# Down projection of a SwiGLU block: eight of eleven row pairs as seven block products instead of eight

## The chip, the cores and the metric

The kernel runs on one core of a Trainium2 chip. The metric is the device time of one execution in microseconds (us); the time before is 926.69 us, the median of three runs that lie between 925.08 and 927.98 us. The core has a matrix engine (TensorE, PE in the profile, with its weight loads as PEld), VectorE (DVE), ScalarE (ACT), GpSimd (POOL) and SyncE (SP), which issues most DMA transfers. TensorE multiplies a stationary 128x128 operand by a moving one of up to 512 columns and adds the product up in PSUM banks of 128x512 fp32; the other engines work from SBUF and PSUM.

## The reference

One encoder layer on 512 tokens of width 1024, in fp32, then a final RMS norm:

```
h  = rms_norm(x, g_mix);  z = h @ w_in            # gates, latent q/kv, mLSTM streams, memory queries
merged = g0 * (o_mla @ w_branch[0]) + g1 * (o_ml @ w_branch[1]) + g2 * (o_mem @ w_branch[2])
x  = x + merged @ w_out
h2 = rms_norm(x, g_ffn)
x  = x + (silu(h2 @ w_ffn_gate) * (h2 @ w_ffn_up)) @ w_ffn_down      # 1024 -> 2816 -> 1024
out = rms_norm(x, g_final)
```

`o_mla` is latent attention (8 heads), `o_ml` a bidirectional mLSTM, `o_mem` attention to 256 memory tokens. The change concerns the last product, `act @ w_ffn_down`: 512 tokens by 2816 by 1024. Its 2816 rows are 22 tiles of 128, taken as 11 pairs ("chunks").

## The kernel before

**Precision.** Every product of two fp32 matrices is made of three fp32r matmuls: each operand is split into a high part (ScalarE copies it into fp32r, L85 or L88) and a low part (VectorE subtracts, L86 or L89), and `mm3` (L101 to L106) adds high x high, low x high and high x low in one bank. `wload` (L91) loads a weight tile of 128x1024 through a raw tile and splits it; raw tiles have two buffers, split ones three.

**Stages.** First the memory keys, then memory attention and mLSTM, then the latent projections (`latent_units`, L703) and latent attention (`mla_units`, L774). Beside these the generator `fill` supplies gate and branch products (`merge_branch`, L225). There the tiles of `merged` are summed: branch product times gate on VectorE (L242), and the sum into `merged` on GpSimd (L243). Then follow the output projection, the second norm, and the feed-forward stage (L947 to L1022), which writes its 22 activation tiles: the first six (`EARLY`) stay in SBUF split, the other sixteen go to a DRAM tile `act_dr`. The first three feed-forward tiles are plain products; the other nineteen (`ffn_first` to `ffn_third`) already use seven block products where eight would be plain, with sums of weight blocks made on VectorE.

**Down projection.** `projection` (L893) takes the two column halves of 512 in turn. In each half every chunk gives, for each of four token tiles, two row tiles of three matmuls: 24 matmuls with 512 columns. The activation is the stationary operand, the weight the moving one. In half 0 `act_load` (L1036) fetches the two activation tiles of a chunk and splits them. In half 1 the last three chunks' weights are kept (`wd_t`) so that each token tile can be finished, normalised and stored in turn (`store`, L1055); there the last token tile is done in two pieces of 256 columns.

**Order of the work.** The program is written as loops; a planner replays it on a timeline of its own and fixes from that each engine's order, preferring what is written first among what is ready. Engines then take their instructions strictly in that order and wait on semaphores. SBUF tiles live in pools that are laid over one another in time: a tile in a new pool must wait for the last use of the old tiles at its place. The pools touched here are `fs`, `ht` and `fg` (feed-forward work tiles, `th` and `u` in `fs`), released at L1023, and `fin` (L1027), which takes their place.

Of the kernel before, what the change touches and what calls it, by code (L numbers as in the profile page):

```python
# [11 lines left out]
F32 = mybir.dt.float32  # L12
F32R = mybir.dt.float32r
I32 = mybir.dt.int32
AF = mybir.ActivationFunctionType
# [22 lines left out]
EARLY = 6  # L38
NEG = -1.0e30
# [21 lines left out]
def block_kernel(ctx, tc, x, mem, pos, inv, g_mix, mem_g, g_ffn, g_final, g_q, g_kv, gate_bias,  # L61
# [17 lines left out]

    def bcast_rows(t, src):  # L80
        nc.gpsimd.dma_start(out=t, in_=src.partition_broadcast(P))
# [26 lines left out]
    def bank(pool):  # L108
        return pool.tile([P, 512], F32, name=pool.name, tag=pool.name)

    def rsqrt_mean(pool, ss, n, count, tag):
# [3 lines left out]
        nc.gpsimd.tensor_tensor(out=r, in0=v, in1=mhalf[:, :n], op=ALU.pow)  # L115
        return r
# [61 lines left out]
    with ExitStack() as mix:  # L178
# [46 lines left out]
        def merge_branch(order, b, o_hi, o_lo, ths, spare=None):  # L225
# [6 lines left out]
            for m in range(KD):  # L232
# [236 lines left out]
        act_mark = []  # L469
# [85 lines left out]
        def head(pr, u, hn):  # L555
# [5 lines left out]
            def make(j):  # L561
                e = lp.tile([P, 640], F32, name="e", tag="e", bufs=3)
                nc.sync.dma_start(out=e, in_=a_dr[h, j].partition_broadcast(P))
# [270 lines left out]

        run(latent_units(), fill, 0.0)
# [3 lines left out]
        run(mla_units(oa_hi, oa_lo), fill, 0.9)  # L839
# [188 lines left out]
    act_hi = fin.tile([P, NF - EARLY, S], F32R, name="act_hi")  # L1028
    act_lo = fin.tile([P, NF - EARLY, S], F32R, name="act_lo")

    def act_side(c):
        if 2 * c < EARLY:
            return early[0], early[1], 2 * c
        return act_hi, act_lo, 2 * c - EARLY

    def act_load(c):  # L1036
        for f in (2 * c, 2 * c + 1):
            if f >= EARLY:
                a = acte.tile([P, S], F32, name="act", tag="act", bufs=2)
                nc.sync.dma_start(out=a, in_=act_dr[f - EARLY])  # L1040
                split(act_hi[:, f - EARLY], act_lo[:, f - EARLY], a, scale=-0.5)

    last = tc.alloc_tile_pool(name="last", bufs=1, side="right")
    wd_t = [[last.tile([P, 1024], F32R, name=f"wd{c}{i}") for i in range(2)] for c in range(3)]
# [4 lines left out]
    def hold_down(lead):  # L1049
        return [wload(w_fd[1, c], into=wd_t[c - lead]) for c in range(lead, NF // 2)]  # L1050

    def gain_low(t):
        nc.gpsimd.tensor_tensor(out=xg[t][:, :H], in0=x2[t][:, :H], in1=gfin_b[:, :H], op=ALU.mult)

    def store(t, r):  # L1055
        rows = slice(t * P, (t + 1) * P)
        A.activation(xg[t][:, :H], xg[t][:, :H], AF.Copy, scale=r)
        nc.scalar.dma_start(out=out[rows, :H], in_=xg[t][:, :H])
        n = H // 2 if t == NT - 1 else H
        for c0 in range(H, D, n):  # L1060
            cols = slice(c0, c0 + n)
# [86 lines left out]
```

## Time and profile before

| | us |
|---|---|
| median of three runs | 926.69 |
| profiled execution, its own time | 925.3 |
| its span | 923.4 |
| TensorE busy | 905.1 |
| VectorE busy | 636.1 |
| ScalarE busy | 509.2 |
| GpSimd busy | 85.2 |

The profile is of one execution. Busy time of TensorE counts overlapping matmuls once, and the granted clock is 0.999 of full speed over the span. A group row gives what an engine did at one line: how often, how long in total and on average, and what ended the idle time ahead of it. A timeline row gives start, length and engine of an instruction (or of several like it, with their count), and in brackets how long the engine idled before and what released it. The profiled execution is 1.39 us below the median.

### The profile page before, as it was taken

Reading aid. Unit: us, or ns where it says so; the run is one execution under the profiler, and the core shown is the slowest. Engines: PE = TensorE matmul, PEld = TensorE weight load, DVE = VectorE, ACT = ScalarE, POOL = GpSimd, SP = SyncE. Lnnn points to the kernel's source line nnn. Section 1 sums busy time; section 2 is a strip of 40 time slices with the busy share of each in tenths; the row PEclk is TensorE's granted clock in tenths of the full one; section 3 lists DMA queues with packets and bytes.
Section 4 is the critical chain, followed back from the end, with each engine's and each line's share of the span. In section 5 each row is a group of like instructions: output and inputs, shape, how many; then the busy total and the mean of one; then the engine's idle time right before and its main releaser. Section 6 shows DMA issues by size and latency. Waiting matters only on the chain.

```text
span 923.4 us, 13931 instructions
## 1 busy us (share of the span) xinstructions
PE 905.1 (98%) x5282; PEld 787.7 (85%) x5282; DVE 636.1 (69%) x1088; ACT 509.2 (55%) x896; POOL 85.2 (9%) x139
## 2 busy tenths in 40 slices
PE   7998999999999999999999999999999999999997
PEld 5987787878888788888888879999999999988886
DVE  5768968888684856677553855989898988354323
ACT  8565676686653456677574445545454545244222
POOL 2001002121111101001000500000000000000200
PEclk9999999999999999999999999999999999999999
DMA  7421244434432122121224250423434431365322
GB/s 274 161 75 47 77 133 125 157 121 140 140 111 92 50 86 83 40 87 60 78 69 160 90 191 17 160 93 125 149 115 127 159 115 69 105 225 162 106 76 91
DMA packets 36675, 104.82 MB, mean 114 GB/s; under 512 B 5169, under 2 KB 7537, under 8 KB 36609
## 3 DMA queue, kind: packets, MB, share of 16 engines
q1 hardware_dynamic: 34560, 99.65, 32.4%
q0 software_dynamic: 1184, 3.24, 1.0%
q10 hardware_dynamic: 864, 1.06, 0.3%
q8 instruction: 41, 0.67, 0.3%
q14 instruction: 26, 0.21, 0.1%
HBM read 97.55 MB, written 6.37 MB: 113 GB/s over the span
## 4 chain that ended last, share of the span: by engine, by line
PE 90%; DVE 4%; DMA 2%; ACT 1%; issue 1%; POOL 0%; POOLq 0%; DVEq 0%; SPq 0%; ACTq 0%
PE pg L104 17%; PE pg L106 17%; PE pg L105 17%; PE po L104 7%; PE po L106 7%; PE po L105 7%; PE psc L104 2%; PE psc L105 2%; PE psc L106 2%; PE ptp L818 2%; DVE w_lo L86 1%; PE ppv L588 1%; PE ppv L587 1%; DMA raw<-w_out_d 1%; PE ppv L586 1%
## 5 line engine op out<-in xcount | busy, mean ns | idle before, releaser
L86 DVE TENSOR_TENSOR w_lo<-raw,w_hi 128x1024 fp32r<-128x1024 f32 (+3 forms) x112 | 126.0, 1127 | 92.4 <-ACT w_hi L85 90.7
L104 PE MATMUL pg<-h_hi,w_hi 128*128 128x512 f32 (+1 forms) x476 | 175.2, 369 | 0.8 <-DVE q_lo L89 0.6
L105 PE MATMUL pg<-h_lo,w_hi 128*128 128x512 f32 (+1 forms) x476 | 175.6, 369 | 0.0
L106 PE MATMUL pg<-h_hi,w_lo 128*128 128x512 f32 (+1 forms) x476 | 175.1, 368 | 0.3 <-DVE w_lo L86 0.3
L85 ACT ACTIVATE w_hi<-raw 128x1024 fp32r<-128x1024 f32 (+3 forms) x112 | 107.0, 958 | 104.4 <-PE pg L105 57.2
L104 PEld LDWEIGHTS pg<-h_hi,w_hi 128*128 128x128 f32 x476 | 89.6, 188 | 15.4 <-DVE q_lo L89 0.8
L106 PEld LDWEIGHTS pg<-h_hi,w_lo 128*128 128x128 f32 x476 | 89.5, 188 | 14.8 <-DVE w_lo L86 0.7
L105 PEld LDWEIGHTS pg<-h_lo,w_hi 128*128 128x128 f32 x476 | 89.5, 188 | 13.7
L571 ACT ACTIVATE e<-e,ccol 128x512 f32<-128x512 f32 (+3 forms) x64 | 32.3, 554 | 28.2 <-DMA e<-a_dr 27.6
L1073 DVE TENSOR_REDUCE nm<-psc 128x1 f32<-128x512 f32 (+1 forms) x48 | 27.7, 596 | 19.9 <-PE psc L106 19.5
L576 DVE TENSOR_TENSOR e<-e,psc 128x512 f32<-128x512 f32 (+3 forms) x64 | 29.1, 482 | 17.5 <-POOL e L574 14.6
L1076 ACT ACTIVATE pn<-psc,nm 128x512 f32<-128x512 f32 (+1 forms) x48 | 29.4, 614 | 17.6 <-DVE nm L1073 17.6
L85 ACT ACTIVATE w_hi<-rawab 128x1024 fp32r<-128x1024 f32 x19 | 20.1, 1059 | 29.0 <-PE pg L105 17.4
L574 POOL TENSOR_SCALAR_AFFINE_SELECT e<-e 128x128 f32<-128x128 f32 x64 | 24.0, 384 | 121.5 <-ACT e L571 110.2
L104 PE MATMUL po<-h_hi,w_hi 128*128 128x256 f32 (+1 forms) x116 | 33.8, 291 | 1.4 <-ACT w_hi L85 1.4
L86 DVE TENSOR_TENSOR w_lo<-rawab,w_hi 128x1024 fp32r<-128x1024 f32 x19 | 23.2, 1222 | 16.1 <-ACT w_hi L85 16.0
L1079 ACT ACTIVATE pn<-pn,rs 128x512 f32<-128x512 f32 (+1 forms) x48 | 29.8, 651 | 7.7 <-DVE rs L1078 7.5
L105 PE MATMUL po<-h_lo,w_hi 128*128 128x256 f32 (+1 forms) x116 | 33.7, 290 | 0.0
L106 PE MATMUL po<-h_hi,w_lo 128*128 128x256 f32 (+1 forms) x116 | 33.6, 290 | 0.0
L86 DVE TENSOR_TENSOR s_lo<-e,s_hi 128x640 fp32r<-128x640 f32 x32 | 26.1, 825 | 4.3 <-ACT s_hi L85 2.6
L105 PE MATMUL po<-w_lo,act_hi 128*128 128x512 f32 (+1 forms) x74 | 27.4, 375 | 0.0
L85 ACT ACTIVATE w_hi<-s 128x1024 fp32r<-128x1024 f32 x19 | 20.1, 1059 | 12.9 <-PE pg L105 9.9
(511 smaller groups left out, 2565.3 us busy)
## 6 DMA issues: line engine op xcount, KB each, us to landing
raw<-w_zt_d SPq DMA_DIRECT2D x46, 512.0 KB, 3.4
raw<-w_fd_d SPq DMA_DIRECT2D x22, 512.0 KB, 3.4
e<-a_dr SPq DMA_DIRECT2D x32, 320.0 KB, 3.4
rawab<-w_fg_d SPq DMA_DIRECT2D x19, 512.0 KB, 3.8
rawab<-w_fu_d SPq DMA_DIRECT2D x19, 512.0 KB, 4.7
raw<-w_br_d SPq DMA_DIRECT2D x12, 512.0 KB, 3.5
raw<-w_out_d SPq DMA_DIRECT2D x8, 512.0 KB, 3.6
act_dr<-u SPq DMA_DIRECT2D x16, 256.0 KB, 3.9
```

What stands on the lines that cost most here:

```text
L85: A.activation(hi, src, AF.Copy)
L86: V.tensor_tensor(out=lo, in0=src, in1=hi, op=ALU.subtract)
L104: mm(ps, wh, ah, start=start and i == 0, stop=False, skip_group_check=more)
L105: mm(ps, wh, al, start=False, stop=False, skip_group_check=more)
L106: mm(ps, wl, ah, start=False, stop=stop and i == n - 1, skip_group_check=more)
L571: A.activation(e[:, c0:c0 + n], e[:, c0:c0 + n], AF.Exp, bias=ccol[:, j, d, row:row + 1])
L574: nc.gpsimd.affine_select(out=dg, in_=dg, pattern=[[sgn, P]], compare_op=ALU.is_ge, fill=0.0, base=0, channel_multiplier=-sgn)
L576: V.tensor_tensor(out=e[:, c0:c0 + n], in0=e[:, c0:c0 + n], in1=sc[:, t0:t0 + n], op=ALU.mult)
L818: nc.tensor.transpose(tp[:, c * 256 + q * P:c * 256 + (q + 1) * P], pn[q][:, (kt + c) * P:(kt + c + 1) * P], ident)
L1073: nc.vector.tensor_reduce(out=nm, in_=sc, axis=AX.X, op=ALU.max, negate=True)
L1076: nc.scalar.activation(pn, sc, AF.Exp, bias=nm, accum_out=sm)
L1079: nc.scalar.activation(pn, pn, AF.Copy, scale=rs)
```

## The change

Eight of the eleven chunks (chunks 3 to 10) are computed as 2x2 block products: the tokens are cut into two halves of 256, a chunk's 256 rows into its two row tiles, the 1024 columns into two halves. The usual eight block products become seven, on sums of blocks. Three loops over the eight chunks do two, three and two of them, with banks `px`, `py`, `pz`, `pw`; the three early chunks (`C0`) stay plain and stand between the loops. `onto` adds a finished or half-finished bank to the residual `x2`.

The four sums of weight blocks per chunk are made by DMA in DRAM: four plain copies on SP's queue (placed after the last load of the mLSTM's `e` tiles), then on GpSimd's queue two accumulating transfers of 2 MB, two copies and two accumulating transfers of 1 MB, two copies and two more accumulating transfers. The sums of activation blocks (`d`) are four 128x256 VectorE operations a chunk. The activations are no longer kept split; they are loaded once (one block a second time) and split per loop. Raw weight tiles lie alternately in `stage` and in `fin`; three chunks' weights are loaded a second time at the end. The sum into `merged` moves from GpSimd to VectorE.

```diff
@@ merge_branch
-                    nc.gpsimd.tensor_tensor(out=merged[:, m], in0=merged[:, m], in1=th, op=ALU.add)
+                    V.tensor_tensor(out=merged[:, m], in0=merged[:, m], in1=th, op=ALU.add)
@@ beside mla_units
+        def down_sums():
+            groups = range(2)
+            low, high = ([w_fd[u, C0 + 4 * g:C0 + 4 * g + 4] for g in groups] for u in range(2))
+            with tc.issue_after(load_mark[0]):
+                for g in groups:
+                    nc.sync.dma_start(out=t13[g][:, :, 0], in_=low[g][:, :, 0:512])
+                    nc.sync.dma_start(out=t13[g][:, :, 1], in_=high[g][:, :, 512:1024])
+            yield
+            def add(t, src):
+                with tc.issue_after(pool_mark[0]):
+                    nc.gpsimd.dma_start(out=t, in_=src, accum_op=ALU.add)
+            for g in groups:
+                add(t13[g], high[g][:, :, 0:512].unsqueeze(2).to_broadcast([4, P, 2, 512]))
+                yield
...
-        run(mla_units(oa_hi, oa_lo), fill, 0.9)
+        run(beside(mla_units(oa_hi, oa_lo), down_sums()), fill, 0.9)
@@ down projection
+    def acts(c):
+        ab = (acte if c == 0 else fin).tile([P, 2, S], F32, name="ab", tag="ab", bufs=1 if c == 0 else 3)
+        for i in range(2):
+            nc.sync.dma_start(out=ab[:, i], in_=act_dr[2 * c + i])
+        b = ab.rearrange("p f (h c) -> p (f h) c", h=2)
+        a11, a21, a12, a22 = (b[:, i] for i in range(4))
+        d = fin.tile([P, 5, HS], F32, name="d", tag="d", bufs=NC)
+        V.tensor_tensor(out=d[:, 0], in0=a22, in1=a21, op=ALU.subtract)
+        V.tensor_tensor(out=d[:, 1], in0=a21, in1=a11, op=ALU.subtract)
+        V.tensor_tensor(out=d[:, 2], in0=d[:, 0], in1=a11, op=ALU.add)
+        V.tensor_tensor(out=d[:, 3], in0=a12, in1=d[:, 2], op=ALU.subtract)
+        nc.sync.dma_start(out=d[:, 4], in_=act_dr[2 * c + 1][:, HS:])
+        return ab, d
...
+        raw = (stage if raws[0] < 3 or raws[0] % 2 == 0 else fin).tile([P, 1024], F32, name="raw", tag="raw", bufs=2)[:, :n]
...
-    projection(((po,) * 4, (pg, pg, pt), (pt, po)),
-               w_fd, NF // 2, 3, act_side, hold_down, gain_low, store, last, act_load)
+    for c in range(C0):
+        w = weights(w_fd[0, c])
+        for t in range(2):
+            plain(py[t], t, c, w, c == 0, False)
+    for c in range(NC):
+        held[c] = acts(c)
+        w = weights(w_fd[0, C0 + c])
+        a = lhs(held[c][0][:, :, :HS], 2, "a2", -0.5)
+        block(px, a, 0, w, 0, c == 0, c == NC - 1)
+        block(py, a, 1, w, 512, False, c == NC - 1)
...
+    for c in range(NC):
+        g, i = divmod(c, 4)
+        w13 = weights(t13[g][i].rearrange("p i c -> p (i c)"))
+        s = lhs(held[c][1][:, 0:3], 3, "a3", 0.5)
+        block(pw, s, 0, w13, 0, c == 0, c == NC - 1)
+        block(pz, s, 1, w13, 512, c == 0, c == NC - 1)
+        w2 = weights(t24[g][i, :, 0])
+        block(px, s, 2, w2, 0, False, c == NC - 1)
...
+    for c in range(NC):
+        g, i = divmod(c, 4)
+        w = weights(w_fd[1, C0 + c][:, 512:1024], t24[g][i, :, 1])
+        a = lhs(held[c][1][:, 3:5], 2, "a2", -0.5)
+        block(pw, a, 0, w, 0, False, False)
+        block(pz, a, 1, w, 512, False, False)
```

`block` makes six matmuls: two token tiles of three.

## Rows read from the trace of the kernel before

**Rows 1.** The page: busy time of the engines, then the chain that ended last.
```profile
PE 905.1 (98%) x5282; PEld 787.7 (85%) x5282; DVE 636.1 (69%) x1088; ACT 509.2 (55%) x896; POOL 85.2 (9%) x139
PE 90%; DVE 4%; DMA 2%; ACT 1%; issue 1%; POOL 0%; POOLq 0%; DVEq 0%; SPq 0%; ACTq 0%
```
**Rows 2.** Stretches: their length, each engine's busy us (instructions), clock, DMA share, GB/s.
```profile
345.00:420.00 75.00, 75.00 (x402) 64.29 (x401) 52.08 (x98) 53.64 (x111) 5.40 (x4) 1.00 0.21 66
530.00:545.00 15.00, 13.99 (x66) 11.57 (x65) 6.96 (x9) 5.87 (x8) 0.57 (x1) 1.00 0.68 228
797.00:810.00 13.00, 13.00 (x70) 11.24 (x69) 3.85 (x7) 2.45 (x6) 0.57 (x1) 1.00 0.37 117
810.00:852.00 42.00, 42.00 (x187) 34.76 (x186) 21.00 (x25) 18.96 (x24) 0.00 (x0) 1.00 0.63 202
852.00:906.00 54.00, 54.00 (x284) 46.42 (x283) 15.69 (x20) 12.84 (x19) 6.03 (x4) 1.00 0.23 78
```
**Rows 3.** Timeline of TensorE: first and last of 55 like matmuls, then two 256-wide.
```profile
524.91 0.39 PE L104 MATMUL po<-w_hi,mg_hi 128*128 128x512 f32 x1
537.15 0.39 PE L104 MATMUL po<-w_hi,mg_hi 128*128 128x512 f32 x1
...
876.51 0.28 PE L104 MATMUL pt<-w_hi,act_hi 128*128 128x256 f32 x1
876.87 0.28 PE L104 MATMUL pt<-w_hi,act_hi 128*128 128x256 f32 x1
```
**Rows 4.** Groups by shape: count, busy us, mean ns, idle before; the last from the feed-forward stage.
```profile
L86 DVE TENSOR_TENSOR w_lo<-raw,w_hi 128x1024 fp32r<-128x1024 f32 x17 | 21.0, 1233 | 35.2 <-ACT w_hi L85 35.0
L85 ACT ACTIVATE w_hi<-raw 128x1024 fp32r<-128x1024 f32 x17 | 18.0, 1059 | 34.3 <-PE po L106 27.3 <-DMA raw<-w_fd_d 4.6 <-PE pg L105 2.4
L89 DVE SCALAR_TENSOR_TENSOR act_lo<-act,act_hi 128x512 fp32r<-128x512 f32 x16 | 10.5, 690 | 7.0 <-ACT act_hi L88 6.9
L877 DVE TENSOR_TENSOR x<-po,x 128x512 f32<-128x512 f32 x4 | 2.8, 691 | 1.6 <-PE po L106 1.6
L1012 DVE TENSOR_TENSOR u<-po,u 128x256 f32<-128x256 f32 x18 | 7.5, 416 | 2.7 <-PE po L106 2.7
```
**Rows 5.** Timelines around the end of the feed-forward stage: TensorE, VectorE, SP, ScalarE.
```profile
787.26 0.40 PE L104 MATMUL po<-w_hi,early_h 128*128 128x512 f32 x1
801.23 0.84 PE L104 MATMUL po<-w_hi,early_h 128*128 128x512 f32 x3
804.66 0.28 PE L106 MATMUL po<-h2t4h,a_lo 128*128 128x256 f32 x1
805.45 0.69 DVE L1013 TENSOR_TENSOR u<-th,u 128x512 f32<-128x512 f32 x1
787.47 2.55 SPq L94 DMA_DIRECT2D raw<-w_fd_d  x2
808.58 1.15 ACT L88 ACTIVATE act_hi<-act 128x512 fp32r<-128x512 f32 x2 [4.64 <-DMA act_dr<-u]
```
**Rows 6.** DMA issues: queue, count, KB each, median us from issue to landing.
```profile
raw<-w_zt_d SPq DMA_DIRECT2D x46, 512.0 KB, 3.4
raw<-w_fd_d SPq DMA_DIRECT2D x22, 512.0 KB, 3.4
xt<-x_d SPq DMA_DIRECT2D x4, 512.0 KB, 9.9
```
**Rows 7.** Timelines of SP and ScalarE between the mLSTM and latent attention.
```profile
265.19 0.32 SPq L563 DMA_DIRECT2D e<-a_dr  x1
268.55 20.90 SPq L94 DMA_DIRECT2D raw<-w_zt_d  x4
280.69 1.06 ACT L85 ACTIVATE w_hi<-raw 128x1024 fp32r<-128x1024 f32 x1 [2.55 <-PE pg L105]
281.65 0.58 ACT L216 ACTIVATE th<-pg 128x512 f32<-128x512 f32 x1
```
**Rows 8.** GpSimd's timeline, then the first and last start of the adds to `x`.
```profile
322.62 1.01 POOL L115 TENSOR_TENSOR q_r<-q_v,mhalf 128x4 f32<-128x4 f32 x1
495.31 2.18 POOL L865 DMA_DIRECT2D x<-x_d  x4 [70.68 <-PE pg L106]
...
L877 DVE TENSOR_TENSOR x<-po,x x13: 415/683/693, 542.6 to 917.2; 128x512 f32<-128x512 f32 x11, 128x256 f32<-128x256 f32 x2
```
**Rows 9.** The sum into `merged` on GpSimd, and what TensorE waited for `mg_lo`.
```profile
L243 POOL TENSOR_TENSOR merged<-merged,th x8: 1289/1296/2282, 320.2 to 423.3; 128x512 f32<-128x512 f32 x8
PEld po L106 <- DVE mg_lo L89: 0.3, 1, 0.3
```

More of the change, by code (lines that the diff above doesn't have):

```diff
@@ L78, in block_kernel @@
     nc.gpsimd.memset(ones, 1.0)
+    t13, t24 = ([dram.tile([4, P, 2, 512], F32, name=f"{n}_{g}") for g in range(2)] for n in ("t13", "t24"))
     def bcast_rows(t, src):
@@ L1027, in block_kernel @@
     fin = ctx.enter_context(tc.tile_pool(name="fin", bufs=1))
[L1028 to L1041, printed above, removed]
     last = tc.alloc_tile_pool(name="last", bufs=1, side="right")
-    wd_t = [[last.tile([P, 1024], F32R, name=f"wd{c}{i}") for i in range(2)] for c in range(3)]
+    wd_t = [[last.tile([P, 1024], F32R, name=f"wd{c}{i}") for i in range(2)] for c in range(C0)]
     xg = [last.tile([P, D], F32, name=f"xg{t}") for t in range(NT)]
@@ L1047, in block_kernel @@
     bcast_rows(gfin_b, g_final)
[L1049 to L1055, printed above, removed]
-        rows = slice(t * P, (t + 1) * P)
[L1057 to L1061, printed above, removed]
+    NC = NF // 2 - C0
@@ new lines, in lhs, with weights @@
+    def lhs(src, n, tag, scale):
+        hi, lo = (fin.tile([P, n, HS], F32R, name=f"{tag}{i}", tag=f"{tag}{i}", bufs=2) for i in "hl")
+        split(hi, lo, src, scale=scale)
+        return hi, lo
+    raws = [0]
+    def weights(*srcs):
+        raws[0] += 1
+        n = 512 * sum(2 if src.shape[-1] == 1024 else 1 for src in srcs)
+        raw = (stage if raws[0] < 3 or raws[0] % 2 == 0 else fin).tile([P, 1024], F32, name="raw", tag="raw", bufs=2)[:, :n]
+        o = 0
+        for src in srcs:
+            w = src.shape[-1]
+            nc.sync.dma_start(out=raw[:, o:o + w], in_=src)
+            o += w
+        return wload(None, n=n, raw=raw)
@@ new lines, in block, with plain @@
+    def block(ps, a, i, w, o, first, last):
+        for t in range(2):
+            ts = slice(t * P, (t + 1) * P)
+            mm3(ps[t], [(a[0][:, i, ts], a[1][:, i, ts], w[0][:, o:o + 512], w[1][:, o:o + 512])],
+                start=first, stop=last, more=True)
+    def plain(ps, t, c, w, first, last, cols=slice(0, H)):
+        ts = slice(t * P, (t + 1) * P)
+        mm3(ps, [(early[0][:, 2 * c + k, ts], early[1][:, 2 * c + k, ts], w[0][:, k * H:(k + 1) * H][:, cols],
+                  w[1][:, k * H:(k + 1) * H][:, cols]) for k in range(2)], start=first, stop=last, more=True)
@@ L1062, in store @@
+    def store(t, v, c0, n):
+        r = keep.tile([P, 1], F32, name="f_r", tag="f_r", bufs=2)
+        nc.gpsimd.tensor_tensor(out=r, in0=v, in1=mhalf[:, :1], op=ALU.pow)
+        rows = slice(t * P, (t + 1) * P)
+        done = slice(c0, c0 + H)
+        A.activation(xg[t][:, done], xg[t][:, done], AF.Copy, scale=r)
+        nc.scalar.dma_start(out=out[rows, done], in_=xg[t][:, done])
+        for c1 in range(H - c0, D - c0, n):
+            cols = slice(c1, c1 + n)
             V.scalar_tensor_tensor(out=xg[t][:, cols], in0=x2[t][:, cols], scalar=r, in1=gfin_b[:, cols], op0=ALU.mult, op1=ALU.mult)
@@ new lines, in block_kernel @@
+    for t in range(2):
+        onto(pw[t], 2 + t, H)
+        onto(pz[t], 2 + t, H, ALU.subtract)
+    py = [bank(po) for _ in range(2)]
+    for c in range(C0):
+        w = wload(w_fd[1, c], into=wd_t[c])
+        for t in range(2):
+            plain(py[t], 2 + t, c, w, c == 0, c == C0 - 1)
+    for t in range(2):
+        onto(px[t], 2 + t, H, ALU.subtract)
+        onto(py[t], 2 + t, H)
+        vs[2 + t] = squares(2 + t, H, EPS)
+        gain(2 + t, H)
+    for t in range(2):
+        onto(px[t], t, H, ALU.subtract)
+        onto(px[t], 2 + t, 0)
@@ new lines, in block_kernel @@
+    for c in range(NC):
[4 more added lines that the diff above has]
+        block(pz, a, 1, w, 512, False, False)
+    for t in range(2):
+        for c in range(C0):
+            plain(pw[t], t, c, wd_t[c], False, c == C0 - 1)
+        onto(pw[t], t, H)
+        store(t, squares(t, H, vs[t]), 0, H)
+    ws = [weights(w_fd[0, c]) for c in range(C0)]
```

55 lines of the change are left out of this document (52 added, 3 removed).

## The prediction

> **What bounds the kernel now.** I read the busy times and the chain that ended last first. TensorE is busy for 905.1 of 923.4 us and makes 90% of the chain [rows 1]; no other engine has more than 4% of it. The table by stretch says the same of each stage that the change touches: in latent attention, at the end of the feed-forward stage and in both halves of the down projection TensorE has no idle time, at full clock, while VectorE is busy 3.85 of 13, 21.0 of 42 and 15.7 of 54 us [rows 2]. So a matmul taken away is worth its spacing, and a wait that reaches TensorE is lost in full.
>
> **What is removed.** The down projection has 11 chunks x 2 halves x 24 = 528 matmuls of 512 columns. After it, the plain chunks have 3 x 48 = 144, and each product chunk 7 products x 2 token tiles x 3 = 42, so 8 x 42 = 336: 480 in all, 48 fewer. The spacing in a full stream is (537.15 - 524.91) / 54 = 0.2267 us [rows 3], so 48 x 0.2267 = 10.9 us. The last token tile was cut into pairs of 256 columns in half 1, 66 pairs; now only 18 pairs are. A pair costs 2 x 0.12 = 0.24 us [rows 3], 0.013 more than one matmul: 48 x 0.013 = 0.6 us. Together 11.5 us, all on TensorE and on the path.
>
> **The sum into `merged`.** Sixteen additions leave GpSimd (1.3 to 2.3 us each) and come to VectorE, at about 0.69 us for 128x512 [rows 9, 4]. Half of them stand in latent attention, where VectorE has 23 us free in 75 [rows 2], and TensorE waits for none. In the other half the chain to the output projection gets shorter, but TensorE waited there only 0.3 us for its end [rows 9]. I take a gain of 0.3; the ends are a gain of 0.3 and, should VectorE's queue delay softmax work, a loss of 1.
>
> **The first loop of the new projection.** This is where I expect the loss. Per chunk TensorE does 12 matmuls, 2.72 us. VectorE does the low part of 1024 weight columns (1.23), that of 512 activation columns (0.69) and four 256-wide sums (4 x 0.416 = 1.67): 3.59 us [rows 4]. ScalarE needs 1.06 + 0.63 and is no limit. So VectorE sets the pace, as it did nowhere in the old projection. Its work for the loop is 8 x 3.59 + 1.23 for the third plain chunk = 30.0 us.
>
> How much of that lies under earlier matmuls? Before, 39 early plain matmuls were put between the last feed-forward products, which end at 804.66 [rows 5]. The plain chunks of the first pass and the loop have 36 + 96 = 132; with no wait the other 93 would end at 804.66 + 93 x 0.2267 = 825.7. VectorE can begin with chunk 0 and its sums at about 797, since these tiles take the place of feed-forward tiles that are done by then, and it has other work of 3.85 - 1.23 = 2.6 us there [rows 2]: 797 + 2.6 + 30.0 = 829.6, and the last chunk's 2.72 us follow: 832.3, or 6.6 us late. A second limit gives nearly the same. The third raw weight tile of the new projection is the first tile in `fin`, where `th` lay, and VectorE reads `th` until 806.1 [rows 5]. Its load (3.4 us) and high part (1.06) make the first matmul possible at 810.6 [rows 4, 6]. TensorE by then has only 24 plain matmuls and chunk 0 to put in between, so it runs dry near 804.0, and the feed-forward end can come up to 3 us earlier for it: 3.5 to 6.5 us idle. VectorE goes on with sums meanwhile, so the two overlap and don't add. The lower end of the loop's cost is 2 (the planner puts sums of late chunks behind their weights, 2 x 1.67 saved, and TensorE finds other work); the upper end is 13 (VectorE first gets to the new work at 804, once the feed-forward tiles are free). I take 6.0, next to the two estimates.
>
> The loop also loads 0.25 x 2 + 0.13 + 0.5 = 1.18 MB a chunk. The highest rate shown is 228 GB/s at a share of 0.68, or 335 GB/s for a full one [rows 2]; that makes 3.5 us a chunk, close to VectorE's 3.59, so the transfers are a second wall at the same place. It is counted in the upper end.
>
> **The other loops.** In the second, VectorE has 1.23 + 0.97 (768 columns, between the two rows) + 0.69 = 2.9 us a chunk against 18 matmuls, 4.08 us; in the third 1.23 + 0.69 = 1.9 against 2.72. At the turn into the second, four additions to `x2` of 0.69 us [rows 4] come on top for a VectorE that is still behind: its queue is 2.9 + 2.8 - 4.1 = 1.6 us late once. I take 1.0 (0 to 3). The three weight tiles loaded again at the end, 3 x 1.23 us, lie under 72 plain matmuls. The end after the last matmul keeps its steps: add, square, root on GpSimd, scale, store. Zero, within 0.5.
>
> **The weight sums in DRAM.** The four copies on SP's queue, 4.2 MB, are ready at once, so I expect them behind the last `e` load at 265.2, ahead of the gate weights from 268.55 on [rows 7]. Loads on that queue follow one another: four loads of 512 KB issued together land after 9.9 us where one alone takes 3.4 [rows 6]. At 335 GB/s the copies hold it for 12.5 us; if a byte read in DRAM and written there counts twice, for 25. The load of 268.55 is split at 280.69, 8.7 us after it would land [rows 6, 7]; behind that, TensorE has another gate product of 24 matmuls, 5.4 us, before it misses a bank that ScalarE frees. So 14.1 us are covered: 0 at one end, 25 - 14.1 = 10.9 at the other. I take 0.5, near the copy's lower end, since no row of this kernel shows a transfer from DRAM to DRAM.
>
> The Trainium skill speaks of such copies (DMA: Bandwidth & Descriptors, Latency and other measured facts): it gives about 207 GB/s for well-laid copies between HBM tensors. By that the copies would take an estimated 20 us; that is 6 us above the cover, and the sum would be 926.8 us on its own time. No trace here shows such a copy yet.
>
> The ten transfers on GpSimd start after the root at 322.6 and each waits for the one before, in order, with GpSimd's later work behind them: the loads of `x`, issued at 495.3 before, and first needed by the addition at 542.6 [rows 8]. So the chain may last some 215 us. It writes 4 x 1 MB by copies and 8 MB by accumulation; at 335 GB/s that is 38 us, and if an accumulated byte is moved three times, 25 + 75 = 100 us, with some 5 us of landing for each of ten: 90 to 150 us. Both ends fit, and latent attention uses a DMA share of only 0.21 [rows 2], so I count nothing; should the chain outlast 215 us, each us more is lost.
>
> **The sum.** On the profiled execution's own time: 925.3 - 11.5 - 0.3 + 6.0 + 1.0 + 0.5 = 921.0 us. The median of the three runs stands 1.4 above that execution, so I predict 922.4.
>
> **The rivals.**
> - *VectorE's work is hidden.* The planner lets the sums slip into the second loop, where VectorE has 1.2 us free a chunk. For it: in 797 to 806 and in loop two there is room for all of it [rows 2]. Against it: the sums are written ahead of the splits of the same chunk. Loop 1.5, turn 0: 925.3 - 11.8 + 1.5 = 915.0, with 1.4: 916.4.
> - *The loop eats the gain.* VectorE starts late, and the transfers at 3.5 us a chunk fall in with it: loop 10, turn 1.5: 925.5, with 1.4: 926.9. For it: both limits lie above TensorE's 2.72. Against it: VectorE and the queue are nearly idle ahead of the loop.
> - *Slower: the copies block SP's queue.* If they hold it for 25 us, a gate weight lands 16.3 us after the time at which ScalarE needs it, ScalarE stands still with its bank releases behind it, and TensorE loses 10.9: 921.0 - 0.5 + 10.9 + 1.4 = 932.8. It decides against the change from 14.1 + 4.8 = 19 us of queue time on. For it: nothing is cheaper to mistime than a transfer that no row shows. Against it: 8.7 us of lead on every gate weight.
> - *Slower still: the copies run on four engines.* Their outermost dimension counts four chunks. If a transfer is dealt out by that dimension, four of 16 engines carry it, 12.5 us become 50, and TensorE loses 50 - 14.1 = 35.9: 957.8. Against it: the four blocks of 128 rows are evenly spaced and can be walked as 512 rows. The Trainium skill has this rule (DMA: Bandwidth & Descriptors, Rules for kernel authors): an outermost dimension below 16 confines a transfer to that many engines. Whether it bites depends on how the pattern is folded, which no row shows.
>
> **How the numbers follow.** Forecast 0.43 (919 to 925.5), hidden 0.20, eaten 0.20, queue 0.12, four engines 0.05. A measurement of this kernel tells about 0.3% from no change, that is 923.9 and 929.5. Faster: hidden 0.20 and three quarters of the forecast, 0.32: 0.52. Same: the rest of the forecast, 0.11, and most of eaten, 0.17: 0.28. Slower: 0.03 + 0.12 + 0.05 = 0.20. The range takes in the hidden case and eaten with its upper half: 915 to 931.
>
> **What would show it.** Right: matmuls down by 48 plus 48 from undone pairs; in the first loop VectorE near full and TensorE waiting on low parts of weights or activations for 4 to 8 us in all; near 804 to 810 a wait on a weight load; no wait on a DMA between 265 and 495; the loads of `x` issued as before. Wrong: TensorE without a gap through the first loop; gaps between 270 and 295 with ScalarE waiting on a gate weight; the additions to `x` after the output projection waiting on their loads.

## The result and the profile after

The changed kernel takes 933.27 us (median of 7 runs, 931.75 to 938.99) against 926.69 (by now also 7 runs, 925.08 to 927.98): a ratio of 1.0080 (1.0056 to 1.0104), 0.8% slower. 922.4 and "faster" were predicted, in a range of 915 to 931. The profiled execution took 935.17 us, 933.5 of them its span.

The page after, which answers to [rows 1]: busy times and the chain; below it TensorE's longest wait (us in total, times, longest).
```profile
PE 902.7 (97%) x5186; PEld 780.8 (84%) x5186; DVE 685.8 (73%) x1175; ACT 532.4 (57%) x923; POOL 73.1 (8%) x133
PE 84%; DMA 6%; DVE 4%; ACT 3%; issue 2%; POOL 1%; POOLq 0%; DVEq 0%; SPq 0%; ACTq 0%
```
```profile
PE po L107 <- ACT w_hi L88: 9.6, 2, 9.0
```
TensorE lost 96 instructions, as worked out (48, and 48 from the undone pairs). But its chain share fell from 90 to 84%, and that of DMA rose from 2 to 6%. Of the transfers on the path, 16.5 us are a gate weight behind the new copies and 6.5 the turn into the projection; 25.5 are loads of `e` in the mLSTM, whose code is the same, so the share alone tells little. Walking both traces along TensorE's matmuls, the changed one is 3.9 us behind at 265 us (2.7 of it in 80 to 86, where this execution's granted clock stood at 0.50, in a stage that the change doesn't touch), 4.5 at 328, 10.3 at 399, 8.8 at 582, 7.2 at 793, and 10.1 at the end. Two places lose: latent attention, and the turn from the feed-forward stage to the projection.

**Latent attention.** Stretches of the changed kernel (columns as in [rows 2]):
```profile
330.00:400.00 70.00, 66.62 (x329) 55.19 (x329) 43.02 (x81) 41.79 (x81) 9.05 (x10) 0.98 1.02 237
345.00:350.00 5.00, 3.06 (x9) 1.90 (x10) 3.53 (x8) 5.00 (x10) 0.66 (x1) 0.89 1.12 206
```
GpSimd's timeline and the DMA issues there answer to [rows 8] and [rows 6]; the issue line by itself is that of the heads' weights in the kernel before, over its whole execution, and the last line is a wait in 330 to 400:
```profile
328.49 3.81 POOL L851 DMA_DIRECT2D t<-w_fd_d  x2
389.89 1.03 POOL L851 DMA_DIRECT2D t<-w_fd_d  x1 [2.32 <-DMA t<-t]
505.64 2.17 POOL L906 DMA_DIRECT2D x<-x_d  x4 [114.73 <-PE pg L109]
```
```profile
t<-w_fd_d SPq DMA_DIRECT2D x4, 1024.0 KB, 13.9
t<-w_fd_d POOLq DMA_DIRECT2D x2, 2048.0 KB, 23.6
t<-t POOLq DMA_DIRECT2D x4, 1024.0 KB, 9.6
t<-w_fd_d POOLq DMA_DIRECT2D x4, 1024.0 KB, 13.4
raw<-w_uq_d SPq DMA_DIRECT2D x4, 192.0 KB, 5.5
```
```profile
raw<-w_uq_d SPq DMA_DIRECT2D x8, 192.0 KB, 2.3
```
```profile
ACT w_hi L88 <- DMA raw<-w_uq_d: 5.8, 2, 3.9
```
The chain of GpSimd transfers is over some 75 us after it began (the last is issued at 389.89 and lands about 13 later), well ahead of the loads of `x`, which waited for TensorE alone. But while it runs the DMA share is 1.02, the weight loads of the heads take 5.5 us instead of 2.3, ScalarE waits for them and TensorE behind it: 3.4 us idle in the stretch, and a granted clock of 0.89 where it had waited most.

The four copies on SP were issued at 269.14 to 271.36, and the gate weight behind them is split at 289.00 instead of 280.69 [rows 7]. ScalarE's instruction just ahead of it is 3.9 us late already, so 4.4 of the 8.3 us are new:
```profile
272.40 19.27 SPq L97 DMA_DIRECT2D raw<-w_zt_d  x3
289.00 1.06 ACT L88 ACTIVATE w_hi<-raw 128x1024 fp32r<-128x1024 f32 x1 [6.95 <-DMA raw<-w_zt_d]
```
TensorE had other work under most of it: between 265 and 328 the walk loses 0.6 us.

**The turn into the projection.** Stretches, and then TensorE, VectorE, SP and ScalarE, against [rows 2, 5]:
```profile
797.00:810.00 13.00, 11.77 (x81) 10.76 (x79) 4.05 (x9) 1.16 (x3) 0.22 (x1) 1.00 0.21 77
810.00:820.00 10.00, 2.27 (x5) 1.64 (x6) 5.33 (x10) 4.00 (x5) 0.36 (x1) 0.66 0.82 260
820.00:830.00 10.00, 10.00 (x38) 8.10 (x38) 9.49 (x17) 5.69 (x7) 0.00 (x0) 0.83 1.03 389
830.00:847.00 17.00, 17.00 (x77) 14.08 (x76) 15.64 (x29) 8.78 (x12) 0.00 (x0) 1.00 0.84 298
```
```profile
808.49 0.28 PE L109 MATMUL po<-h2t4h,a_lo 128*128 128x256 f32 x1
817.73 1.22 PE L107 MATMUL po<-w_hi,early_h 128*128 128x512 f32 x2 [8.96 <-ACT w_hi L88]
820.12 0.63 PE L109 MATMUL po<-w_hi,early_l 128*128 128x512 f32 x1
820.55 0.63 PE L107 MATMUL po<-w_hi,early_h 128*128 128x512 f32 x1
841.41 0.62 PE L107 MATMUL po<-w_hi,a3h 128*128 128x512 f32 x2
847.31 0.61 PE L109 MATMUL po<-w_hi,a2l 128*128 128x512 f32 x2
809.27 0.69 DVE L1054 TENSOR_TENSOR u<-th,u 128x512 f32<-128x512 f32 x1
812.36 0.43 DVE L1085 TENSOR_TENSOR d<-ab 128x256 f32<-128x256 f32 x1 [2.40 <-DMA act_dr<-u]
803.38 6.93 SPq L992 DMA_DIRECT2D act_dr<-u  x2
812.41 0.33 SPq L1106 DMA_DIRECT2D raw<-w_fd_d  x1
816.62 2.00 ACT L88 ACTIVATE w_hi<-raw 128x1024 fp32r<-128x1024 f32 x2 [2.29 <-DMA raw<-w_fd_d]
```
The load of the third plain chunk's weights, the first into `fin`, goes out at 812.41, when the last store of `u` has landed, and so does the first sum `d`, though by the order and sizes in the code its tile doesn't lie over `u`. TensorE stands still for 9.0 us: its last feed-forward product is turned into `u` (done at 809.96), `u` is stored (2.3 us to land), the weight is loaded (4.2) and split (1.1). Its next matmuls are 0.43 us apart instead of 0.23, at a granted clock of 0.50 (1.2 GHz) in 818 to 823: 12 of them, some 2.7 us more. Behind that TensorE has no wait up to 848. In 820 to 830 VectorE is busy 9.49 of 10 and the DMA share is 1.03.

From the last feed-forward product to the first addition to `x` (847.3) are 38.8 us. TensorE has 108 matmuls of the first pass there, 24.5 us at 0.2267, and 12 of the second loop (`a3h`, `a3l`) that the planner put ahead of the end of the first, 2.7: the first loop costs the other 11.6, the gap and the low clock. The rest, to the end of the span, is 86.2 us, and 88.9 with those 12; the prediction's sum has some 87 there (a span of 919.1 less a loop that ends at 825.7 + 6.0).

### The profile page after: what moved, and what is told of

The parts are those of the page before. It is cut to its first block, busy times and chain, and to the rows that moved or that the text cites. A ratio compares the mean times of both kernels' runs of the same rounds, so it can differ in the third digit from the quotient of the medians.

```text
span 933.5 us, 13944 instructions
## 1 busy us (share of the span) xinstructions
PE 902.7 (97%) x5186; PEld 780.8 (84%) x5186; DVE 685.8 (73%) x1175; ACT 532.4 (57%) x923; POOL 73.1 (8%) x133
## 4 chain that ended last, share of the span: by engine, by line
PE 84%; DMA 6%; DVE 4%; ACT 3%; issue 2%; POOL 1%; POOLq 0%; DVEq 0%; SPq 0%; ACTq 0%
PE pg L107 15%; PE pg L108 15%; PE pg L109 15%; PE po L108 7%; PE po L107 7%; PE po L109 7%; DMA e<-a_dr 3%; PE psc L107 2%; DMA raw<-w_zt_d 2%; PE psc L108 2%; PE psc L109 2%; PE ptp L823 1%; PE pt L108 1%; PE pt L109 1%; PE pt L107 1%
## 5 line engine op out<-in xcount | busy, mean ns | idle before, releaser
L89 DVE TENSOR_TENSOR w_lo<-raw,w_hi 128x1024 fp32r<-128x1024 f32 (+3 forms) x131 | 142.7, 1091 | 65.8 <-ACT w_hi L88 62.6
L107 PE MATMUL pg<-h_hi,w_hi 128*128 128x512 f32 (+1 forms) x476 | 177.5, 374 | 1.8 <-ACT up L283 0.8
L88 ACT ACTIVATE w_hi<-raw 128x1024 fp32r<-128x1024 f32 (+3 forms) x131 | 123.1, 945 | 96.1 <-PE pg L108 43.7
L108 PEld LDWEIGHTS pg<-h_lo,w_hi 128*128 128x128 f32 x476 | 90.5, 190 | 13.9
L156 DVE TENSOR_TENSOR s<-rawab 128x1024 f32<-128x1024 f32 x19 | 23.2, 1223 | 5.3 <-DMA rawab<-w_fu_d 5.2
## 6 DMA issues: line engine op xcount, KB each, us to landing
t<-w_fd_d SPq DMA_DIRECT2D x4, 1024.0 KB, 13.9
t<-w_fd_d POOLq DMA_DIRECT2D x2, 2048.0 KB, 23.6
```

The costliest lines, as they stand in the source:

```text
L88: A.activation(hi, src, AF.Copy)
L89: V.tensor_tensor(out=lo, in0=src, in1=hi, op=ALU.subtract)
L107: mm(ps, wh, ah, start=start and i == 0, stop=False, skip_group_check=more)
L108: mm(ps, wh, al, start=False, stop=False, skip_group_check=more)
L156: V.tensor_tensor(out=s31, in0=ab[:, 0:4:3], in1=ab[:, 2:3].to_broadcast([P, 2, 512]), op=ALU.add)
```

## The experiments

All ran on one core, each beside runs of the kernel before on the same chip; ratios are to these, with 95% intervals. Multiplied by 927, 0.1% is 0.9 us.

**First: which part.** Theory: the projection's tiles open late. Rivals: VectorE's pace in the loop; the weight sums' transfers.

*Third raw weight outside `fin`.*
```
-        raw = (stage if raws[0] < 3 or raws[0] % 2 == 0 else fin).tile(...)
+        raw = (stage if raws[0] < 4 or raws[0] % 2 == 0 else fin).tile(...)
```


> Only the third plain chunk's raw weight tile moves from the new pool to the old staging pool, so its load need not wait for the feed-forward pool. Theory pool: the 9.0 us in which TensorE waits after the feed-forward stage come from the new pool, whose first tiles wait as a whole for the last store of u. Then 12 matmuls (2.7 us) come into that gap, the split of chunk 0's weight no longer stands behind the late one, the gap falls to 2 to 5 us, the half clock after it mostly goes, and the time falls by 6 to 10 us from the changed kernel's 933.3. Theory VectorE pace: the first loop ends when VectorE has done its 30 us of work, which still starts at the same time; then the gap shrinks but VectorE gives the loop the same end, and the time falls by no more than 3 us.

934.88 us, 1.0069 (1.0049 to 1.0089). TensorE's timeline:
```profile
812.51 0.80 PE L107 MATMUL pg<-w_hi,a2h 128*128 128x512 f32 x1 [4.55 <-ACT a2h L91]
819.93 1.22 PE L107 MATMUL pg<-w_hi,a2h 128*128 128x512 f32 x2 [2.93 <-ACT w_hi L88]
```
The plain chunk no longer waits, and about the same time is lost in front of chunk 0 and chunk 1, as the rival had it (no more than 3 us faster). The waits fall from 9.0 to 7.5 us, but there are two of them now, with matmuls at the lower clock behind each (0.50 in 820 to 825): of the 36.8 us from the last feed-forward product to the first addition, 4.6 go to that, against 2.7 in the changed kernel. The one load was not the cause.

*No weight sums.* `down_sums()` is left out, and the loops load plain blocks of the same size.
```
-        run(beside(mla_units(oa_hi, oa_lo), down_sums()), fill, 0.9)
+        run(mla_units(oa_hi, oa_lo), fill, 0.9)
```


> The changed kernel without the fourteen transfers that sum weight blocks in DRAM; the loops load blocks of the plain weights of the same size in their place, so the output is not the reference's. Theory transfers: the 5.9 us lost in latent attention come from transfers that saturate the DMA engines, so that weights land late; the time falls by 5 to 7 us from 933.3. Theory VectorE: the loss there comes from the sum into merged on VectorE or from another order of the work; the time falls by under 2 us and the stretch from 330 to 400 us keeps its loss.

925.5 us, 0.9979 (0.9964 to 0.9995): the sums cost 1.0% here, 9 us. The wait of 8.7 us for `w_hi` ahead of the third plain chunk stays.

*The sums alone*, added to the kernel before and not used.

> The kernel before with the fourteen transfers added, their results unused. Theory transfers: 5 to 8 us slower than before (932 to 935), lost between 330 and 400 us, with ScalarE waiting on loads of w_uq and w_br. Theory VectorE: within 1.5 us of before.

935.08 us, 1.0085 (1.0055 to 1.0114): 8 us by themselves.

*The merged sum alone.*
```
-                    nc.gpsimd.tensor_tensor(out=merged[:, m], in0=merged[:, m], in1=th, op=ALU.add)
+                    V.tensor_tensor(out=merged[:, m], in0=merged[:, m], in1=th, op=ALU.add)
```


> The kernel before with only the sum into merged moved from GpSimd to VectorE. Theory transfers: latent attention is unchanged and the way to the output projection gets shorter, 0 to 2 us faster than before. Theory VectorE: 3 to 6 us slower, lost in latent attention.

924.73 us, 0.9964 (0.9950 to 0.9977); run again later (below) 0.9966 (0.9954 to 0.9979). It gains 3.2 us, ten times the term of the sum. TensorE's waits of the kernel before in 515 to 600, and in 600 to 760, are gone in it:
```profile
PE po L104 <- DVE x L877: 1.0, 1, 1.0
...
PE po L104 <- ACT w_hi L85: 1.4, 2, 0.8
```
The second, at 600 to 760, lies in the feed-forward stage, whose code is the same while the order of its matmuls differs between the two traces; so part of the gain is another order of the instructions, and not the addition's own price.

So the parts are: sums +8 to +9, merged sum -3.2, and the new projection, without sums against merged sum alone (0.9979 to 0.9964), +1.4 us, where -4.5 was predicted; the two intervals leave some 2 us either way.

**Second: inside the loop, and another place for the sums.** *The activation sums on GpSimd.*
```
-        V.tensor_tensor(out=d[:, 0], in0=a22, in1=a21, op=ALU.subtract)
+        nc.gpsimd.tensor_tensor(out=d[:, 0], in0=a22, in1=a21, op=ALU.subtract)
 (and the three behind it)
```


> The changed kernel with the four activation sums of each chunk (128x256) on GpSimd instead of VectorE. Theory 'handoff' (TensorE loses its time because the new tiles open late, with the feed-forward pools, and not because VectorE is slow afterwards): 932 to 935 us, within 1.5 of the changed kernel's 933.3, and the same gap of some 9 us before the third plain chunk. Theory 'VectorE pace' (3.59 us a chunk against 2.72 of TensorE): VectorE has 1.92 us a chunk left, 8 x 1.67 = 13.4 us less in the loop, and the kernel comes to 926 to 929. Theory 'transfers' (DMA share 0.9 to 1.0 in the loop): 932 to 935, and the gap after chunk 0 stays, ended by loads.

935.46 us, 1.0087 (1.0073 to 1.0100), no gain. But it took nothing off VectorE, which is busy 33.4 of 40 us in 810 to 850 against 33.2 with the sums on it. Groups there: two of the changed kernel, then three of this one (ns min/median/max, first and last start):
```profile
L89 DVE TENSOR_TENSOR w_lo<-raw,w_hi x12: 684/1219/1226, 818.0 to 849.7; 128x1024 fp32r<-128x1024 f32 x11, 128x512 fp32r<-128x512 f32 x1
L92 DVE SCALAR_TENSOR_TENSOR a2l<-ab,a2h x8: 679/684/691, 813.4 to 843.0; 128x512 fp32r<-128x512 f32 x8
```
```profile
L89 DVE TENSOR_TENSOR w_lo<-raw,w_hi x12: 1210/1752/1759, 815.9 to 849.4; 128x1024 fp32r<-128x1024 f32 x11, 128x512 fp32r<-128x512 f32 x1
L92 DVE SCALAR_TENSOR_TENSOR a2l<-ab,a2h x8: 1005/1222/1226, 811.9 to 842.1; 128x512 fp32r<-128x512 f32 x8
L1085 POOL TENSOR_TENSOR d<-ab x8: 713/1192/1719, 810.9 to 848.3; 128x256 f32<-128x256 f32 x8
```
Each of these VectorE instructions takes some 0.53 us longer beside GpSimd's sums, and a GpSimd sum up to 1.72 us where it takes 0.71 alone. So the run doesn't tell the theories apart. The Trainium skill (SBUF — State Buffer, SBUF: two separate sides) has the rule: the two engines share a pair of ports as a lock, and a VectorE instruction with two inputs in SBUF is held while GpSimd reads. These durations agree with it.

*`th` and `u` kept, so that nothing of the projection lies over them.*
```
-    fs = tc.alloc_tile_pool(name="fs", bufs=1)
+    fs = ctx.enter_context(tc.tile_pool(name="fs", bufs=1))
-        raw = (stage if raws[0] < 3 or raws[0] % 2 == 0 else fin).tile(...)
+        raw = stage.tile(...)
```


> The changed kernel with the pool that holds th and u kept open to the end, and all raw weights in the two tiles outside it, so that no tile of the projection lies where th or u lay and none has to wait for the last stores of u. Theory 'handoff': the first sum d begins at about 808.5 instead of 812.4 and the third plain chunk no longer waits, 3 to 5 us faster than the changed kernel: 928 to 930. Theory 'VectorE pace': VectorE begins as much earlier, but keeps its 30 us of work: 930 to 932, with the matmul gap moved behind chunk 0. Theory 'transfers': two raw tiles instead of four and the same bytes in the same stretch, 932 to 936.

952.73 us, 1.0269 (1.0247 to 1.0291), missed by all three. The first sum `d` does start at 809.83, and the first loop ends at 841.6 instead of 847.3; but the two other loops and the end take 106.6 us instead of 86.2, with eight waits for a weight. Two raw tiles are too few. Nor is the gap gone:
```profile
809.96 0.50 PE L107 MATMUL pg<-w_hi,a2h 128*128 128x512 f32 x1 [1.66 <-ACT a2h L91]
819.01 0.80 PE L107 MATMUL pg<-w_hi,a2h 128*128 128x512 f32 x1 [6.04 <-ACT a2h L91]
```
Chunk 0 runs at once, from the block that lies outside; chunk 1's block is loaded into `fin`, which opens with the last product.

*As that, and the 36 plain matmuls of the other half ahead of the loop* (`plain(pz[t], 2 + t, ...)` on the free `pt` banks).

> As the kernel with th and u kept, and besides the 36 plain matmuls of the other column half for token tiles 2 and 3 put ahead of the first loop (three weight tiles are split once more for that, 3 x 1.23 us of VectorE in the feed-forward stage). They need no tile that opens late: 36 x 0.2267 = 8.2 us of TensorE work for the gap. Theory 'handoff': most of the gap is bridged, 6 to 9 us faster than the changed kernel: 924 to 927. Rival: these matmuls are missed where they stood, between the second and the third loop, and VectorE, still behind, stops TensorE there: 928 to 932.

958.21 us, 1.0330 (1.0311 to 1.0349), slower by 6 us than that run. The gap at 810 to 820 is bridged, but the matmuls are missed where they stood, as the rival had it, and with two raw tiles at a higher price than it named:
```profile
911.06 1.22 PE L107 MATMUL po<-w_hi,a2h 128*128 128x512 f32 x2 [11.97 <-ACT w_hi L88]
```

*The weight sums in the feed-forward stage*, behind its first stored block (the expectation says fourth by mistake).

> The changed kernel with the weight sums (four copies on SP's queue, ten transfers on GpSimd's) issued in the feed-forward stage, after its fourth stored block, instead of during latent attention. Theory 'place' (the transfers delay the weight loads of latent attention, which come one by one when they are needed): 925 to 928, with TensorE without gaps at 330 to 400 us. Theory 'bytes' (they take the DMA engines wherever they stand): 932 to 936, with the loads of the feed-forward weights late instead, and TensorE waiting on s or a tiles of lhs_side.

953.60 us, 1.0262 (1.0239 to 1.0286): 17 us worse than in latent attention. "Place" was wrong the other way: this stage loads weights at a share of 0.40 already, and with the sums TensorE is busy 71.46 of 80 us in 680 to 760, at a DMA share of 1.01.

**Third: what opens the loop.** *`th` and `u` kept, with four raw tiles* (`ab` with two buffers, `junk` with one).

> The changed kernel with th and u kept, as before, but with all four raw weight tiles again (one buffer less for ab and one for the squares make the room). With two raw tiles the first loop ended at 841.6 us of the span, against 847.3 in the changed kernel, and the rest took 20 us longer. Theory 'handoff': the first loop keeps its gain of 5 to 6 us, the rest takes as long as in the changed kernel: 926 to 929 us. Rival 'order': the time that the second and third loop lost came from another order of the work and not from the missing raw tiles; they stay slow: 940 to 950.

936.14 us, 1.0095 (1.0078 to 1.0111). The end behind the first loop is back to 85.6 us, so it was the raw tiles. But the first loop ends at 847.3, as in the changed kernel:
```profile
809.53 0.50 PE L107 MATMUL pg<-w_hi,a2h 128*128 128x512 f32 x1 [1.24 <-ACT a2h L91]
819.04 1.22 PE L107 MATMUL pg<-w_hi,a2h 128*128 128x512 f32 x2 [6.49 <-ACT w_hi L88]
```
The theory of the stores fell: whichever tile waits, the loop's loads begin with the end of the feed-forward stage, and chunk 1 runs at 819.

*The same, with the plain matmuls behind the last feed-forward product.*
```
+    pe_end = next(i for i in reversed(nc.cur_bb.bb.instructions) if i.engine == mybir.EngineType.PE)
+        with tc.issue_after(pe_end):
             for t in range(2):
                 plain(py[t], t, c, w, c == 0, False)
```


> As the run with th and u kept and four raw tiles, and the 36 plain matmuls of the first pass issued behind the last feed-forward matmul instead of among them. Theory 'handoff': the feed-forward stage ends up to 5 us earlier, so the loads that wait for its tiles go out earlier, and the 8.2 us of plain matmuls lie under them: 3 to 6 us faster than that run, 921 to 925. Rival: the last feed-forward products wait for their own sums and splits, which the plain matmuls had covered, so TensorE idles there instead: within 1.5 of that run.

931.26 us, 1.0031 (1.0018 to 1.0044): 6 us faster than that run. The last product starts at 801.89, the loads go out from 802.8, the 36 matmuls lie under them. From the last product to the first addition pass 41.2 us with 144 matmuls, where that run took 39.3 with 108: the loss beside them falls from 14.8 to 8.5. What is left (stretches, then TensorE: one wait, and all for `a2h`):
```profile
810.00:820.00 10.00, 9.73 (x42) 7.50 (x41) 9.77 (x16) 7.22 (x9) 0.00 (x0) 1.00 1.01 376
820.00:830.00 10.00, 6.25 (x20) 4.66 (x20) 7.05 (x14) 2.10 (x3) 0.00 (x0) 0.83 0.92 328
830.00:840.00 10.00, 8.19 (x35) 6.15 (x34) 6.71 (x13) 4.87 (x7) 0.00 (x0) 1.00 0.42 134
```
```profile
825.81 0.50 PE L107 MATMUL pg<-w_hi,a2h 128*128 128x512 f32 x1 [3.75 <-ACT a2h L91]
PE pg L107 <- ACT a2h L91: 5.4, 2, 3.7
```
ScalarE waits there for `ab<-act_dr`: at a DMA share of 1.01 and 0.92 the blocks come late.

*The same without the activation sums*; ScalarE copies the block in their place.
```
-        V.tensor_tensor(out=d[:, 0], in0=a22, in1=a21, op=ALU.subtract)  (and three)
+        A.activation(d[:, 0:4], b, AF.Copy)
```


> As the run with the plain matmuls behind the feed-forward stage, with the four activation sums of each chunk left out: ScalarE copies the block (one 128x1024 instruction) where VectorE formed them, so the output is not the reference's. VectorE has 13.4 us less in the first loop and nothing on GpSimd beside it. Theory 'VectorE pace' (3.59 us a chunk against TensorE's 2.72): 4 to 7 us faster than that run. Theory 'handoff': VectorE's share is under other work once the loop starts early: within 1.5.

928.70 us, 1.0007 (0.9992 to 1.0022): 2.2 us less, between the two theories. VectorE's sums cost something here, but less than its pace had been given.

*Only the four copies of the weight sums.*

> The kernel before with only the four copies of 1 MB on SP's queue, none of the ten transfers on GpSimd's; the results are not used. The weight sums as a whole cost 7 to 8 us when added alone. Theory 'accumulations' (the transfers on GpSimd's queue, at a DMA share above 1, delay the weight loads of latent attention): the copies alone cost at most 1.5 us, 926 to 929. Theory 'copies' (SP's queue is held): 4 us or more, 931 to 935.

929.76 us, 1.0018 (1.0005 to 1.0031): 1.7 of the 8 us. Latent attention with all the sums, and with the copies alone, each added to the kernel before:
```profile
330.00:400.00 70.00, 66.74 (x341) 55.73 (x340) 41.70 (x76) 44.36 (x87) 12.66 (x13) 1.00 1.04 244
```
```profile
330.00:400.00 70.00, 70.00 (x359) 59.31 (x359) 42.98 (x84) 44.86 (x89) 5.65 (x4) 1.00 0.21 72
```

**Fourth: transfers or VectorE, burst or bytes.** All on the run with the plain matmuls behind. *One activation block for chunks 1 to 7.*

> As the run with the plain matmuls behind the feed-forward stage, with the activation block of chunks 2 to 7 not loaded (the tile of chunk 1 is used again, so the output is not the reference's): 0.63 MB a chunk in the first loop instead of 1.13. Theory 'transfers' (after the feed-forward end the loads of the loop run at a DMA share near 1, and TensorE waits for an activation block): the wait of 3.7 us for a2h at 825.8 goes, 4 to 8 us faster than that run's ratio. Theory 'VectorE pace' (its 3.59 us a chunk): within 1.5, since VectorE does all its work.

928.69 us, 1.0010 (0.9994 to 1.0025): 2 us, neither the 4 expected nor a clear no, and the intervals overlap. From the last feed-forward product to the first addition it takes 35.4 us, against 41.2 in the run with all loads; but 2.7 of the 5.8 are the 12 matmuls of the second loop, which now stand behind the addition, and 2.6 were lost again before the projection in this execution. Inside, the wait for `a2h` is gone, and a new one stands in its place:
```profile
820.45 0.50 PE L108 MATMUL pg<-w_lo,a2h 128*128 128x512 f32 x1 [3.88 <-DVE w_lo L89]
```
With all blocks at hand at once, 18 sums, most of them of later chunks, stood on VectorE ahead of that `w_lo`. From 821 on TensorE has only one wait, 0.5 us at the end.

*The same without the activation sums.*

> The same, and without the activation sums as well (ScalarE copies the block; the output is not the reference's). The sums alone were worth 2.3 us. If transfers and VectorE are two separate walls of about one height, both together give more than the two alone added: 9 to 13 us faster than the run with both. If they act one behind the other, about the sum of the two. TensorE then runs through the first loop with no wait over 1 us.

929.65 us, 1.0020 (1.0001 to 1.0040), no faster, against both answers: now ScalarE copied six blocks, 5.77 us, ahead of the weights of chunk 1, and TensorE waited 6.4 us for `w_hi`. It measured the queue's order, and tells nothing of the two walls.

*The weight sums spread.* Ten transfers become twenty of half the size, each behind a small GpSimd copy that waits for the next block of latent attention.
```
+                    ov, rs = unit[0]
+                    pool_mark[:] = [nc.gpsimd.tensor_copy(out=tick[rs], in_=ov[rs, :1]).ins]
                 with tc.issue_after(pool_mark[0]):
                     nc.gpsimd.dma_start(out=t, in_=src, accum_op=ALU.add)
```


> As the run with the plain matmuls behind the feed-forward stage, with the ten transfers of the weight sums cut in halves and issued one at a time, each behind a small GpSimd copy that waits for the next block of latent attention (some 9 us apart), so that they fill half of the time and not all of it. Theory 'burst' (weight loads of latent attention come too late because the transfers follow one another without a break, at a DMA share of 1.0): 3 to 6 us faster than that run, and no slower than the kernel before. Theory 'bytes' (each byte costs what it costs, wherever it falls): within 1.5 of that run.

925.98 us, 0.9982 (0.9967 to 0.9998): 4.5 us faster, as "burst" had it. The bytes are the same; walking from the run with the plain matmuls behind to this one, 4.6 us are won between 331 and 399, and TensorE has no gap there:
```profile
330.00:400.00 70.00, 70.00 (x355) 58.59 (x354) 44.95 (x88) 44.43 (x88) 7.17 (x10) 1.00 0.50 115
400.00:520.00 120.00, 120.00 (x624) 101.22 (x623) 74.07 (x135) 76.42 (x150) 16.62 (x33) 1.00 0.64 163
```

**Fifth: the loads again, without a change of VectorE's work; and the best version.** *As that, and the fifth block of `d` loaded in the second loop.*
```
-        nc.sync.dma_start(out=d[:, 4], in_=act_dr[2 * c + 1][:, HS:])
...
         block(px, s, 2, w2, 0, False, c == NC - 1)
+        with tc.issue_after(w_mark[0]):
+            nc.sync.dma_start(out=held[c][1][:, 4], in_=act_dr[2 * c + 1][:, HS:])
```


> As the run with the weight sums spread, with the fifth block of d (the plain quarter that only the third loop reads, 0.13 MB a chunk) loaded in the second loop instead of the first. Theory 'transfers' (the first loop waits for loads at a DMA share near 1): 1.0 MB less in it, at the 340 GB/s measured there 3 us; 1.5 to 3 us faster than that run, 923 to 924.5. Theory 'VectorE pace' (its 28.7 us of work for the loop): within 1. Against the kernel with only the merged sum moved (ratio 0.9964): level with it, within 0.2%.

922.76 us (6 runs, 921.26 to 926.24), 0.9946 (0.9927 to 0.9965): 3.3 us faster, a little more than the bytes at 340 GB/s. The traces show less of it in the loop. TensorE's waits for `a2h`, in the run with the sums spread and then here:
```profile
PE pg L109 <- ACT a2h L93: 3.0, 1, 3.0
PE pg L109 <- ACT a2h L93: 2.9, 2, 2.3
```
From the last product to the first addition 38.5 us become 37.7, with 144 matmuls (32.6 us) in both. Of the 4.2 us between the two spans 2.4 lie ahead of the projection, where nothing was changed. So the gain of the run is measured, and that all of it comes from the loads put off is not shown.

*The merged sum alone again*, beside it.

> The kernel before with only the sum into merged moved to VectorE, run again beside the mended version of the whole change. Its first ratio was 0.9964: again 0.995 to 0.998. If the projection gains after all its mends, the other run is below it; if the gain of the matmuls is used up, the two agree within 0.2%.

924.82 us, 0.9966 (0.9954 to 0.9979). So the whole change, with its loop opened earlier, its sums spread and one load put off, has the lowest median found, 5 us below the kernel before; 3 of the 5 are the merged sum's. The intervals of the two best overlap at 0.9954 to 0.9965, so that the new projection gains at all is not shown.

## Why the prediction was wrong

- *Removed matmuls*: right. The count is exact, and everything behind the first loop took 88.9 us, with the 12 matmuls drawn ahead, against some 87. So the second loop, the turn into it, the reloaded weights and the end were sized rightly to some 2 us.
- *The weight sums*: the step that failed most. The copies were sized well: the gate load issued behind them at 272.40 landed 16.5 us later where 3.4 are usual [rows 6], so they held it up for 13 us (12.5 taken, 20 by the second estimate), and the 0.5 cost 0.6 in the walk and 1.7 in the run with the copies alone. Of the ten transfers on GpSimd the prediction asked only whether their chain ends before the loads of `x`, and it did, in 75 us where 90 to 150 were bounded. "Both ends fit, and latent attention uses a DMA share of only 0.21 [rows 2], so I count nothing" is where it went wrong: a mean share of 0.21 says that there is room on average, not that a load which is needed in 4 us lands in 4 us. At a share of 1.02 a head's weights of 192 KB took 5.5 us to land, where they had taken 2.3. The price is some 6 us, shown by the copies alone, the sums alone and the spread run.
- *The first loop*: 6.0 us were taken, and 11.6 were lost in the profiled execution, 9.0 in one gap and the rest at the lower clock behind it. What failed is the time at which the loop's tiles open. The prediction let VectorE begin at 797, "since these tiles take the place of feed-forward tiles that are done by then"; the first sum began at 812.4, behind the last store of `u`, and at 809.4 to 809.8 where `th` and `u` were kept. So a tile here opens when the pools beneath its own are done, not when the bytes beneath it are, and no weight past the two tiles outside and no block past chunk 0's could be loaded before the last product. The prediction's second limit, the load of the third plain chunk (3.5 to 6.5 us idle), names the wait that came, but dates it by VectorE's last read of `th`: it leaves out the store (2.3 us), and lets chunk 0 fill in, whose split parts lie in `fin` too. VectorE's pace, on which the 6.0 rest, stopped TensorE nowhere: behind the gap there is no wait up to 848. The transfers, which the prediction counted only in its upper end of 13, show once that gap is filled: 7.5 us in front of chunks 0 and 1 with the third weight outside, 5.4 for `a2h` with the plain matmuls behind. (The terms of its 1.18 MB a chunk add up to 1.13 as they are written; nothing hangs on it.) The late opening is shown by the run with the plain matmuls behind (-6 us against the same tiles without it). VectorE's sums were worth 2.2, measured with the loop already earlier. What the transfers behind the opening cost isn't separated further: the two runs with fewer loads gave 2.0, with intervals that overlap, and 3.3, of which the traces show 0.8 in the loop.
- *The merged sum*: right in sign, 3.2 us instead of 0.3, of which 2.6 us can be seen as waits gone behind latent attention. Why the planner's order in the feed-forward stage got better isn't settled.
- *Rivals*: "the loop eats the gain" was the nearest for the loop; "copies block SP's queue" hit the total of 932.8 by luck, since the time was lost elsewhere: the gate weight was split 4.4 us late and TensorE lost 0.6. The copies did not run on four of 16 engines: in 272 to 283 the DMA share is 1.01, at 303 GB/s.

In terms of the sum: -0.3 became -3.2, 0.5 became +8, and -4.5 for the projection became between +1.4 (runs without sums) and +2.7 (what 1.0080 leaves).

## What to carry to other kernels

A background transfer is not free because the mean share is low: ask which loads are issued just before they are needed, and leave pauses between the pieces of the transfer. At a change of stage, ask for each new tile when the pool beneath it is released, and keep work that needs none of them for the time just after the release, not before it. And before moving work to a neighbouring engine, check that the two don't hold each other up.

## What the runs showed of the hardware

- Beside each other and the weight loads, at a DMA share of 1.02, an accumulating transfer from DRAM to DRAM took 13.4 us for 1 MB and 23.6 for 2 MB on GpSimd's queue, a plain one of 1 MB 9.6; four plain ones issued together on SP's queue landed after 13.9 us (medians from issue to landing).
- VectorE instructions with two inputs in SBUF took 0.53 us longer beside GpSimd sums (1.22 to 1.75, 0.68 to 1.22); two additions with one input in PSUM kept their 1.29 us.
- After 9 us without work TensorE's matmuls came 0.43 us apart, at a granted clock of 0.50, until 823.1, 5.4 us after it had begun again.
